# A third pair of feed-forward chunks as block products, on tokens without the norm's factor, in a transformer block on one core

## The chip, the cores and the metric

The kernel runs on one core of a Trainium2 chip. The metric is device time in microseconds of one launch. The profile is of one execution; its span, from the first to the last instruction of the engines, is a little shorter than the time of that execution. TensorE does the matmuls, ScalarE casts, copies and looks up activation functions, VectorE (DVE) does the elementwise work, GpSimd (POOL) some transfers and a little elementwise work, and SyncE (SP) issues most loads.

## The reference

One block over 256 tokens of 1024 channels, in fp32. The hidden width of a feed-forward is 2816.

```python
def rmsnorm(x, g):
    return x * rsqrt(mean(x * x) + 1e-6) * g

def swiglu(h, w_in, w_down):
    gate, up = split(h @ w_in, 2)
    return (silu(gate) * up) @ w_down

x = x + 0.5 * rmsnorm(swiglu(rmsnorm(x, g1), ffn1_w_in, ffn1_w_down), g2)
h = rmsnorm(x, g3)                                   # mixer
q_a, f_a, i_a, g_a, q_b, k_b, v_b, f_b, gates = split(h @ w_in)
a = rmsnorm(gated_recurrence(silu(q_a), f_a, i_a), g4) * silu(g_a)
b = forgetting_attention(q_b, k_b, v_b, f_b)
gA, gB = sigmoid(gates + b_gate)
x = x + rmsnorm((gA * (a @ w_branch_a) + gB * (b @ w_branch_b)) @ w_out, g5)
x = x + rmsnorm(memory_attention(rmsnorm(x, g6), rmsnorm(mem, g7)), g8)
x = x + 0.5 * rmsnorm(swiglu(rmsnorm(x, g9), ffn2_w_in, ffn2_w_down), g10)
```

## The kernel before

**Split weights.** Each product of two fp32 operands is three matmuls, of the high parts and low parts of both (high by high, high by low, low by high), summed in one bank. A weight unit is 128 x 1024 (512 KB). `load_split` has SP load it into a `raw` tile (4 buffers), ScalarE cast the high part `hi` (L137) and DVE subtract it for the low part `lo` (L138); 8 buffers each for `hi` and `lo`. The tokens stand transposed, in eight blocks of 128 channels x 256 tokens, as high and low part too (`hT`, `lT`, made by `gain_split` with the norm's gain, L271 and L272). The norm's factor per token (the rsqrt) is left out of them and multiplied in after the product, as `r2[h]` for the two halves h of 128 tokens.

**A feed-forward (`ffn`)** goes through 11 chunks (`NFF`) of 256 hidden columns. For an ordinary chunk, four units of `w_in` are met with each half of the tokens, 24 matmuls of 512 columns a half (`act_tok`; `act_first` does both halves side by side, for the first three chunks of the first feed-forward). `act_evac` then takes the Silu of the gate columns on ScalarE and multiplies it on DVE with the up columns to `at`. `flush` puts four transposes of `at` on TensorE and splits the result to `act`. `down(c, h)` multiplies `act` of chunk c and half h with two units of `w_down`, 12 matmuls of 512 columns into the accumulators `acc`, one or two chunks later.

**A pair of chunks as block products (`quad`).** Two chunks can be done together: tokens in 2 halves, channels in 2 halves and hidden columns in 2 chunks make a 2 x 2 by 2 x 2 block product, done with seven products of 12 matmuls in the place of eight. It needs sums of token blocks (`s1` to `s4`, made once by `mixed`) and four sums of weight blocks, T1 to T4. In the first feed-forward the half of the units that is only needed in sums is loaded into `wide` (2 buffers), and DVE makes the sums from `raw` and `wide`: `t1` (L481), `t2` (L482), `t4` (L484) for each half q of the channels, T3 later in place in `wide` (L494). `sum_of(k)` then splits a sum to high and low part (L156, L157). The order on TensorE in a pair is: 24 matmuls on two weight blocks, transposes of a chunk before it, T1's product, `down`, T2's product, `down`, T3's, `down`, and the rest. In the second feed-forward the sums were made between the feed-forwards and are loaded from DRAM. `QUADS_1 = (5, 8)` and `QUADS_2 = (3, 5, 7, 9)` name the first chunk of each pair.

Before the first pair, `mixed` (before) multiplies the tokens with the norm's factor, which must stand as a row: `row_of` makes it by two diagonal matrices and two matmuls with ones. The product of both is split anew to the pair `N`, and chunks behind it use `N` in place of `X` and no factor in `act_evac`.

**The order.** Each engine runs one queue in order; a scheduler lays out the queues from the order in which the program asks for work, with its priorities. `after(n)` puts an instruction right behind the n-th matmul of the program's own log and `issue_after` behind a given instruction. The loads on SP run in the order of the program, each as soon as its buffer is free.

**Start and end.** Eight loads (`head`, into the four `raw` and the two `wide` buffers) bring a block of tokens, of the first weights and the gains together; ScalarE (L713, L271) and DVE split them block by block. `norm_1` loads x and makes the norm's factors, with `rstd_x` for each half. The first feed-forward stands up to about 180 us in the span, mixer and memory attention to about 600, then the second feed-forward to about 775 and the last norm: `post_last` takes the Sqrt on ScalarE (L357), the reciprocal and two steps of a root's refinement on DVE, and updates x in three parts, two on DVE (L376) and one by ScalarE and POOL (L373 and on).

## Time and profile before

| | |
|---|---|
| time, median of 3 runs | 785.01 us (785.0 to 785.46) |
| the profiled execution | 785.17 us, span 783.4 us |
| TensorE (PE) busy | 774.3 us, 99% of the span |
| weight load (PEld) | 669.9 us, 86% |
| DVE | 646.2 us, 82% |
| ScalarE (ACT) | 468.4 us, 60% |
| POOL | 48.4 us, 6% |
| DMA | 193.61 MB, mean 247 GB/s |

How to read it: a row of a group names line, engine, operation, out<-in, shape, count, then busy time and mean ns of one, then idle time in front of it with what ended it. A row of the timeline has the start in us from the span's start, the duration, the engine, line and operation; a square bracket gives a wait before it and whom it was for; "x2" puts two like instructions in one row, and the duration runs to the end of the last. A row of the windows has start and end, the length, then for PE, PEld, DVE, ACT and POOL the busy time with the count of instructions, then the granted clock, the share of the DMA engines and GB/s. Matmul rows are those of one helper, L93 (`MM`), and are told apart by their tiles.

### The profile page before, as it was taken

How to read it: one execution, taken by the hardware profiler on the slowest of the kernel's cores; microseconds unless marked ns; L12 is line 12 of the kernel's file. 1: busy time of each engine (PE TensorE's matmuls, PEld its weight loads, DVE VectorE, ACT ScalarE, POOL GpSimd, SP SyncE). 2: the span in 40 equal slices, each digit the busy share in tenths (PEclk: the TensorE clock that was granted, in tenths of full speed). 3: DMA queues.
4: the chain of work that ended last, by engine and by line, in shares of the span. 5: the costliest groups of instructions: out<-in, count | busy, mean ns of one | idle time of the engine just before them, and what ended most of it. 6: DMA issues, size and time to landing. Idle time of an engine off the chain costs nothing.

```text
span 783.4 us, 13175 instructions
## 1 busy us (share of the span) xinstructions
PE 774.3 (99%) x5004; PEld 669.9 (86%) x5004; DVE 646.2 (82%) x1004; ACT 468.4 (60%) x704; POOL 48.4 (6%) x81
## 2 busy tenths in 40 slices
PE   9999999999999999999999999999999999999996
PEld 7888888888899999998888888999888888888884
DVE  7889989968798898578777886998787889888864
ACT  7665664756752447347674444744646758677763
POOL 0000000000121100200001221011110000000000
PEclk9999999999999999999999999999999999999999
DMA  9794484476687655753479999579875279899831
GB/s 349 249 327 154 155 309 161 147 233 245 251 305 257 183 191 164 232 212 121 152 278 341 377 338 378 203 275 375 319 226 185 83 261 388 311 314 323 339 122 54
DMA packets 57392, 193.61 MB, mean 247 GB/s; under 512 B 6249, under 2 KB 9713, under 8 KB 57329
## 3 DMA queue, kind: packets, MB, share of 16 engines
q1 hardware_dynamic: 48080, 159.60, 57.9%
q0 software_dynamic: 9104, 33.04, 12.1%
q8 instruction: 39, 0.64, 0.3%
q14 instruction: 25, 0.20, 0.1%
q10 hardware_dynamic: 144, 0.13, 0.0%
HBM read 174.92 MB, written 17.83 MB: 246 GB/s over the span
## 4 chain that ended last, share of the span: by engine, by line
PE 99%; ACT 0%; DVE 0%; issue 0%; DVEq 0%; ACTq 0%
PE mm L93 64%; PE acc L93 28%; PE tr L93 4%; PE tr L395 1%; PE tr L315 1%; PE tr L1067 0%; PE tr L1158 0%; PE tr L1264 0%; ACT L357 0%; PE tr L406 0%; DVEq L1393 0%; DVE xs L376 0%; ACT hT L156 0%; ACT y L357 0%; ACT junk L243 0%
## 5 line engine op out<-in xcount | busy, mean ns | idle before, releaser
L138 DVE TENSOR_TENSOR lo<-raw,hi 128x1024 fp32r<-128x1024 f32 (+1 forms) x228 | 271.3, 1205 | 53.0 <-ACT hi L137 49.2
L137 ACT CAST hi<-raw 128x1024 fp32r<-128x1024 f32 (+1 forms) x228 | 232.1, 1036 | 118.2 <-PE mm L93 69.5
L93 PE MATMUL mm<-lo,hT 128*128 128x512 f32 (+1 forms) x448 | 171.2, 386 | 0.0
L93 PE MATMUL mm<-hi,hT 128*128 128x512 f32 (+1 forms) x448 | 170.7, 385 | 0.0
L93 PE MATMUL mm<-hi,lT 128*128 128x512 f32 (+1 forms) x448 | 170.4, 384 | 0.0
L93 PE MATMUL acc<-hi,act 128*128 128x512 f32 x352 | 113.2, 391 | 0.0
L93 PE MATMUL mm<-hT,hi 128*128 128x256 f32 x384 | 109.0, 284 | 0.1
L93 PE MATMUL mm<-hT,lo 128*128 128x256 f32 x384 | 109.0, 284 | 0.0
L93 PE MATMUL mm<-lT,hi 128*128 128x256 f32 x384 | 108.9, 284 | 0.0
L93 PEld LDWEIGHTS mm<-hi,hT 128*128 128x128 f32 x448 | 84.1, 188 | 16.1 <-ACT hT L271 0.7
L93 PEld LDWEIGHTS mm<-hi,lT 128*128 128x128 f32 x448 | 84.1, 188 | 15.8 <-DVE lT L272 0.5
L93 PEld LDWEIGHTS mm<-lo,hT 128*128 128x128 f32 x448 | 84.0, 188 | 15.0 <-DVE lo L138 0.4
L93 PEld LDWEIGHTS acc<-hi,act 128*128 128x128 f32 x352 | 65.9, 188 | 13.7 <-DVE act L157 0.2
L93 PEld LDWEIGHTS mm<-hT,hi 128*128 128x128 f32 x384 | 73.6, 192 | 0.5 <-issue 0.3
L93 PEld LDWEIGHTS mm<-lT,hi 128*128 128x128 f32 x384 | 73.6, 192 | 0.1
L93 PEld LDWEIGHTS mm<-hT,lo 128*128 128x128 f32 x384 | 73.6, 192 | 0.1
L93 PE MATMUL acc<-lo,act 128*128 128x512 f32 x176 | 69.0, 392 | 0.0
L157 DVE TENSOR_TENSOR lo<-wide,hi 128x1024 fp32r<-128x1024 f32 x40 | 47.9, 1219 | 1.5 <-ACT hi L156 1.1
L156 ACT CAST hi<-wide 128x1024 fp32r<-128x1024 f32 x40 | 41.5, 1052 | 11.5 <-DVE wide L494 7.5
L776 POOL DMA_DIRECT2D sums<-wide x32 | 23.6, 738 | 357.8 <-DVE wide L773 240.8
L93 PEld LDWEIGHTS acc<-lo,act 128*128 128x128 f32 x176 | 33.1, 188 | 6.7
L93 PE MATMUL mm<-hi,sh 128*128 128x512 f32 x96 | 37.5, 390 | 0.0
(243 smaller groups left out, 1126.8 us busy)
## 6 DMA issues: line engine op xcount, KB each, us to landing
raw<-in_wts_dram SPq DMA_DIRECT2D x232, 512.0 KB, 5.1
sums<-wide POOLq DMA_DIRECT2D x32, 512.0 KB, 6.2
wide<-sums SPq DMA_DIRECT2D x32, 512.0 KB, 6.9
wide<-in_wts_dram POOLq DMA_DIRECT2D x28, 512.0 KB, 6.7
wide<-in_wts_dram SPq DMA_DIRECT2D x12, 512.0 KB, 6.4
raw<-in_gf_dram SPq DMA_DIRECT2D x12, 344.0 KB, 4.9
head<-in_head_dram SPq DMA_DIRECT2D x8, 388.0 KB, 5.7
grow<-in_rows_dram SPq DMA_DIRECT2D x4, 512.0 KB, 8.9
```

Source lines behind the costliest of these rows:

```text
L93: log.append(PE.matmul(*args, **kw).ins)
L137: S.copy(h, r)
L138: V.tensor_tensor(out=l, in0=r, in1=h.bitcast(F32), op=ALU.subtract)
L156: S.copy(hi, src)
L157: V.tensor_tensor(out=lo, in0=src, in1=hi.bitcast(F32), op=ALU.subtract)
L315: PE.transpose(ps[:, j * P : (j + 1) * P], src(kb), ident)
L395: PE.transpose(trv[:, j, h * P : (h + 1) * P], ats[c, h][:, j * P : (j + 1) * P], ident)
L776: G.dma_start(sums[u][2 * e : 2 * e + 2, q, :, i * 512 : i * 512 + 512].rearrange("k p n -> p k n"), W[:, e])
```

## The change

- `QUADS_1` has three pairs, (3, 6, 9), in place of two, (5, 8). The eleven chunks are then 0, 1, 2, a pair, 5, a pair, 8, a pair. The last pair is at the end, as in the second feed-forward, and `ffn` treats the end of the first one as it did that of the second (which `down` is left for last differs).
- `mixed` takes the tokens without the norm's factor. `row_of`, the multiplication and the split to `N` are gone from it; it returns the sums alone. `act_evac` always has the factor as Silu's scale and in DVE's product. In the first feed-forward the whole tokens, `full1`, are eight copies by ScalarE out of the `head` tiles, with the gain as scale, asked for behind the last head's low part; in the second, DVE adds high and low part as before.
- In a pair of the first feed-forward `t2` and `t4` of the first half (q = 0) are asked for at once, those of the second half behind the first `down`.
- Smaller: both halves' norm factors are made together (`rstd_pair`, 128 x 2 in place of 128 x 1); the row of gains for the last norm is loaded later; q and G of the mixer take ScalarE's Silu in place of Sigmoid and a product on DVE; in the second feed-forward the Sqrt table is asked for only behind the last Silu of the program (before: behind the Silu of the second half of chunk 10, after which another Silu came); `post_last` has three updates on DVE.

```diff
-QUADS_1 = (5, 8)
+QUADS_1 = (3, 6, 9)
-    def mixed(X, r, back=0):
-        with after(len(log) - 1 - back):
-            row = row_of(r)
-        full = [m4([P, 4, T], n="full") for _ in range(2)]
-        for f, xh, xl in zip(full, X.h, X.l):
-            V.tensor_tensor(out=f, in0=xh.bitcast(F32), in1=xl.bitcast(F32), op=ALU.add)
-            V.tensor_tensor(out=f, in0=f, in1=bc(row, [P, 4, T], 1), op=ALU.mult)
-        N = Pair()
-        for q in range(2):
-            split(N.h[q], N.l[q], full[q])
+    def mixed(X, full):
+        if full is None:
+            full = [m4([P, 4, T], n="full") for _ in range(2)]
+            for f, xh, xl in zip(full, X.h, X.l):
+                V.tensor_tensor(out=f, in0=xh.bitcast(F32), in1=xl.bitcast(F32), op=ALU.add)
...
+    full1 = [m4([P, 4, T], n="full") for _ in range(2)]
+    for kb in range(KB):
+        with tc.issue_after(lo_last):
+            S.activation(full1[kb // 4][:, kb % 4], heads[kb][:, :T], AF.Copy, scale=heads[kb][:, T + 512 + kb : T + 512 + kb + 1])
...
         def act_evac(ps, c, h):
-            if mix:
-                silu = S.activation(sg, ps[:, :FC], AF.Silu)
-            else:
-                silu = S.activation(sg, ps[:, :FC], AF.Silu, scale=r2[h])
-            if c == NFF - 1 and (c, 1 - h) in ats and not first_half:
+            silu = S.activation(sg, ps[:, :FC], AF.Silu, scale=r2[h])
+            if len(ats) == 2 * NFF - 1 and not first_half:
                 with tc.issue_after(silu.ins):
                     S.activation(warm, ones[:, 0:1], AF.Sqrt)
...
+                def rest(W, raws, t1, t2, t4):
+                    V.tensor_tensor(out=t2, in0=t1, in1=W[:, :, 1], op=ALU.add)
+                    for i in range(2):
+                        V.tensor_tensor(out=t4[:, i], in0=t2[:, i], in1=raws[i][:, 512:], op=ALU.add)
...
-                    V.tensor_tensor(out=t2, in0=t1, in1=W[:, :, 1], op=ALU.add)
-                    for i in range(2):
-                        summed = V.tensor_tensor(out=t4[:, i], in0=t2[:, i], in1=raws[i][:, 512:], op=ALU.add).ins
+                        summed = V.tensor_tensor(out=t1[:, i], in0=raws[i][:, :512], in1=W[:, i, 0], op=ALU.add).ins
+                    if q == 0:
+                        rest(W, raws, t1, t2, t4)
...
             down(n_down, 0)
+            if not sums:
+                rest(W, raws, t1, t2, t4)
...
-            down(n_down + 1, 1)
+            if not (last and first_half):
+                down(n_down + 1, 1)
...
-            for c in ends:
+            for c in (NFF - 3, *ends) if done == NFF - 2 else ends:
                 down(c, 1)
...
-        for eng, a, b, queue in ((G, 512, 768, nc.scalar), (V, 0, 512, nc.sync), (V, 768, 1024, nc.sync)):
+        for a, b, queue in ((0, 512, nc.sync), (512, 768, nc.scalar), (768, 1024, nc.sync)):
...
-            if eng is G:
-                S.activation(t, t, AF.Copy, scale=r)
-                G.tensor_tensor(out=xh, in0=t, in1=xh, op=ALU.add)
-            else:
-                V.scalar_tensor_tensor(out=xh, in0=t, scalar=r, in1=xh, op0=ALU.mult, op1=ALU.add)
+            V.scalar_tensor_tensor(out=xh, in0=ts[a // 512][:, a % 512 : a % 512 + b - a], scalar=r, in1=xh, op0=ALU.mult, op1=ALU.add)
```

In all TensorE has 16 instructions fewer, and DVE seven.

**ScalarE at the start, before.** The rows show its queue from the last head tile (`head_94`: high part of the weights, of the tokens) to the first casts of chunk 1 (`raw_203`, `raw_209`):

```order
L713 CAST hi_143<-head_94 128x512
L271 ACTIVATE hT_87<-head_94 128x256
L713 CAST hi_143<-head_94 128x512
L271 ACTIVATE hT_87<-head_94 128x256
L137 CAST hi_204<-raw_203 128x1024
L137 CAST hi_210<-raw_209 128x1024
```

The same place after, where `full_153` and `full_154` are the two halves of the whole tokens:

```order
L725 ACTIVATE full_153<-head_89 128x256
L719 CAST hi_143<-head_94 128x512
L285 ACTIVATE hT_87<-head_94 128x256
L725 ACTIVATE full_153<-head_90 128x256
L719 CAST hi_143<-head_94 128x512
L285 ACTIVATE hT_87<-head_94 128x256
L725 ACTIVATE full_153<-head_91 128x256
L725 ACTIVATE full_153<-head_92 128x256
L725 ACTIVATE full_154<-head_93 128x256 x2
L725 ACTIVATE full_154<-head_94 128x256 x2
L136 CAST hi_214<-raw_213 128x1024
```

All eight copies stand ahead of the first cast of chunk 1 (`hi_214`), two of them between the splits of the last heads.

**DVE in the first pair, before** (chunks 5 and 6). `sum_787`, `sum_788` and `sum_789` are t1, t2 and t4 of q = 0, `sum_810` to `sum_812` those of q = 1; `lo_819` and `lo_823` are the low parts of T1:

```order
L482 TENSOR_TENSOR sum_788<-sum_787,wide_772 128x1024
L422 SCALAR_TENSOR_TENSOR at_729<-mm_702,rstd_317,sg_727 128x256
L484 TENSOR_TENSOR sum_789<-sum_788,raw_773 128x512
L484 TENSOR_TENSOR sum_789<-sum_788,raw_780 128x512
L157 TENSOR_TENSOR lo_807<-raw_803,hi_806 128x1024
L481 TENSOR_TENSOR sum_810<-raw_796,wide_795 128x512
L481 TENSOR_TENSOR sum_810<-raw_803,wide_795 128x512
L157 TENSOR_TENSOR lo_819<-sum_787,hi_818 128x1024
L482 TENSOR_TENSOR sum_811<-sum_810,wide_795 128x1024
L157 TENSOR_TENSOR lo_823<-sum_810,hi_822 128x1024
```

The same place after (chunks 3 and 4). `sum_502` to `sum_504` are the sums of q = 0, `sum_525` is t1 of q = 1, `wide_487` and `wide_510` in place are T3, `act_330` the low part of chunk 2's activations, `lo_531` and `lo_535` the low parts of T1:

```order
L465 TENSOR_TENSOR sum_503<-sum_502,wide_487 128x1024
L498 TENSOR_TENSOR wide_487<-wide_487 128x2x512
L467 TENSOR_TENSOR sum_504<-sum_503,raw_488 128x512
L467 TENSOR_TENSOR sum_504<-sum_503,raw_495 128x512
L156 TENSOR_TENSOR lo_522<-raw_518,hi_521 128x1024
L485 TENSOR_TENSOR sum_525<-raw_511,wide_510 128x512
L485 TENSOR_TENSOR sum_525<-raw_518,wide_510 128x512
L156 TENSOR_TENSOR lo_531<-sum_502,hi_530 128x1024
L498 TENSOR_TENSOR wide_510<-wide_510 128x2x512
L156 TENSOR_TENSOR act_330<-tr_565,act_330 128x512
L156 TENSOR_TENSOR lo_535<-sum_525,hi_534 128x1024
```

`t2` of q = 1 has moved out from between T1's two low parts, and both T3, with one `act`, now stand ahead of the second of them.

**ScalarE at the end, before.** `sg` are Silus, `warm` the call that fetches the Sqrt table, `y` the Sqrt of the last norm:

```order
L417 ACT_TABLE_LOAD
L417 ACTIVATE warm_79<-ones 128x1
L412 ACT_TABLE_LOAD
L412 ACTIVATE sg_8073<-mm_7823 128x256
L156 CAST act_7787<-tr_8077 128x2x128
L156 CAST act_7786<-tr_8130 128x2x128
L243 ACTIVATE junk,ss_1577_8135<-acc_6913 128x512
L243 ACTIVATE junk,ss_1577_8135<-acc_6914 128x512
L243 ACTIVATE junk,ss_1587_8184<-acc_6915 128x512
L243 ACTIVATE junk,ss_1587_8184<-acc_6916 128x512
L357 ACT_TABLE_LOAD
L357 ACTIVATE y_8191<-ss_1587_8184,v_8186 128x1
```

The same place after:

```order
L415 ACTIVATE sg_8018<-keep_7903,rstd_6529 128x256
L415 ACTIVATE sg_8045<-mm_7796,rstd_6705 128x256
L155 CAST act_7760<-tr_8050 128x2x128
L418 ACT_TABLE_LOAD
L418 ACTIVATE warm_79<-ones 128x1
L155 CAST act_7759<-tr_8103 128x2x128
L257 ACTIVATE junk,ss_1560_8108<-acc_6886 128x512
L257 ACTIVATE junk,ss_1560_8108<-acc_6887 128x512
L257 ACTIVATE junk,ss_1570_8157<-acc_6888 128x512
L257 ACTIVATE junk,ss_1570_8157<-acc_6889 128x512
L366 ACTIVATE y_8164<-ss_1570_8157,v_8159 128x1
```

The table load in front of the Sqrt is gone; the Sqrt table is fetched once, behind the last Silu.

67 lines of the change are left out of this document (37 added, 30 removed).

## The prediction

> **What bounds the kernel now.** First the page: the busy line and the chain that ended last.
>
> ```profile
> PE 774.3 (99%) x5004; PEld 669.9 (86%) x5004; DVE 646.2 (82%) x1004; ACT 468.4 (60%) x704; POOL 48.4 (6%) x81
> PE 99%; ACT 0%; DVE 0%; issue 0%; DVEq 0%; ACTq 0%
> ```
>
> TensorE has work nearly all the time and the chain runs on it. A busy TensorE can still hide short waits, so next the windows by stage (x counts instructions) and the timeline of TensorE in the first feed-forward.
>
> ```profile
> 4.00:180.00 176.00, 175.98 (x797) 144.72 (x797) 152.40 (x200) 110.57 (x148) 0.00 (x0) 1.00 0.66 228
> 600.00:775.00 175.00, 175.00 (x796) 143.80 (x795) 146.51 (x202) 119.66 (x166) 0.00 (x0) 1.00 0.69 248
> 62.11 0.40 PE L93 MATMUL mm<-hi,hT 128*128 128x512 f32 x1
> 73.02 0.39 PE L93 MATMUL acc<-hi,act 128*128 128x512 f32 x1
> ```
>
> Both feed-forwards are gapless at granted clock 1.00. Between the two matmuls lie 48 matmuls of 512 columns: 10.91 / 48 = 0.227 us each. So a matmul removed is worth 0.227 us, and any wait that the change brings to TensorE is paid in full. DVE, at 152.4 of 176 us (87%) in the first feed-forward, is the engine that could bring one.
>
> **The change part by part.**
>
> *Matmuls.* A pair of chunks as block products needs 7 x 12 = 84 matmuls in place of 4 x 24 = 96; the third pair therefore removes 12: 12 x 0.227 = **2.72 us**. Tokens without the norm's factor need no broadcast row of it; the two rows that `mixed` made (one per feed-forward) go. Each stands on TensorE like this:
>
> ```profile
> 55.74 0.61 PE L93 MATMUL tr<-diag,ones 128*128 128x128 f32 x4
> 56.11 0.47 PE L93 MATMUL acc<-hi,act 128*128 128x512 f32 x1
> ```
>
> 56.11 - 55.74 = 0.37, twice **0.74 us**. Both terms are sure: 16 matmuls fewer stand on TensorE, and nothing hides work there. [...]
>
> *The tail.* The last Silu now comes before the Sqrt table is fetched, so the table stays, and POOL's share of the last update goes to DVE.
>
> ```profile
> 776.27 0.19 ACT L243 ACTIVATION_READ_ACCUMULATOR junk<-acc 128x1 f32 x1
> 776.49 1.28 ACT L357 ACT_TABLE_LOAD   x1
> 777.11 0.15 DVE L359 TENSOR_TENSOR v<-ss,v 128x1 f32<-128x1 f32 x1
> 777.78 0.29 ACT L357 ACTIVATE y<-ss,v 128x1 f32<-128x1 f32 x1
> 778.11 0.17 DVE L364 RECIPROCAL y<-y 128x1 f32<-128x1 f32 x1 [0.85 <-ACT y L357]
> 778.76 1.61 DVE L376 SCALAR_TENSOR_TENSOR xs<-post,y,xs 128x512 f32<-128x512 f32 x2
> L376 DVE SCALAR_TENSOR_TENSOR xs<-post,y,xs 128x256 f32<-128x256 f32 x1 | 0.9, 946 | 0.0
> L422 DVE SCALAR_TENSOR_TENSOR at<-mm,rstd,sg 128x256 f32<-128x256 f32 x12 | 5.7, 476 | 0.5 <-ACT sg L414 0.4
> ```
>
> Without the load y is ready at 776.8, but DVE only ends v at 777.26; the reciprocal starts at 777.28 in place of 778.11, a gain of 0.83, not 1.28. The update then has three DVE instructions (0.67 to the start of the second, 0.40 more, then 0.48: 1.55) for two that took 1.61 beside POOL. Together **0.9 us** (0.6 to 1.1). [...]
>
> *Start.* ScalarE now also copies the eight token blocks (`full1`), all ahead of the first cast of chunk 1.
>
> ```profile
> 8.16 0.51 ACT L271 ACTIVATE hT<-head 128x256 fp32r<-128x256 f32 x1
> 8.59 0.62 ACT L713 CAST hi<-head 128x512 fp32r<-128x512 f32 x1
> 12.06 0.51 ACT L271 ACTIVATE hT<-head 128x256 fp32r<-128x256 f32 x1
> 12.82 1.05 ACT L137 CAST hi<-raw 128x1024 fp32r<-128x1024 f32 x1 [0.25 <-DMA raw<-in_wts_dram]
> 13.90 5.07 DVE L138 TENSOR_TENSOR lo<-raw,hi 128x1024 fp32r<-128x1024 f32 x4 [0.53 <-ACT hi L137]
> 16.20 0.62 PE L93 MATMUL acc<-hi,hT 128*128 128x512 f32 x2
> 17.10 0.62 PE L93 MATMUL acc<-lo,hT 128*128 128x512 f32 x2
> ```
>
> Such a copy occupies ScalarE 0.43 (8.16 to 8.59). ScalarE is free at 12.06 + 0.43 + 8 x 0.43 = 15.93; the cast ends at 16.98 where TensorE wants it at 16.20 (0.8 late); the low part takes DVE 1.22 more, 18.24 for 17.10: **+1.1 us**. The load behind the cast now waits for the copy of its buffer (about 11.0) and lands by 16.1 at the latest (landing times below), so it adds at most 0.2; behind it on SP's queue wait the loads of chunks 1 and 2 and of x, all wanted more than 4 us later than they land. Bounds 0.8 to 1.4. The second unit is wanted 2.7 us later and is in time.
>
> *The first pair, two chunks earlier.* DVE's order there is all work without a break; its prices, from the first pair of before:
>
> ```profile
> 70.58 0.68 DVE L157 TENSOR_TENSOR act<-tr,act 128x512 fp32r<-128x512 f32 x1
> 71.18 0.47 DVE L422 SCALAR_TENSOR_TENSOR at<-mm,rstd,sg 128x256 f32<-128x256 f32 x1
> 71.57 1.28 DVE L481 TENSOR_TENSOR sum<-raw,wide 128x512 f32<-128x512 f32 x2
> 72.77 1.22 DVE L157 TENSOR_TENSOR lo<-raw,hi 128x1024 fp32r<-128x1024 f32 x1
> 73.91 1.21 DVE L482 TENSOR_TENSOR sum<-sum,wide 128x1024 f32<-128x1024 f32 x1
> 75.04 0.47 DVE L422 SCALAR_TENSOR_TENSOR at<-mm,rstd,sg 128x256 f32<-128x256 f32 x1
> 81.25 1.21 DVE L157 TENSOR_TENSOR lo<-sum,hi 128x1024 fp32r<-128x1024 f32 x1
> 84.35 0.40 PE L93 MATMUL mm<-hi,sh 128*128 128x512 f32 x1
> 38.90 0.40 PE L93 MATMUL acc<-hi,act 128*128 128x512 f32 x1
> ```
>
> Start to start: 1.14 for 1024 elements, 0.60 for 512, 0.40 for 256. In before the second low part of T1 is there at 82.5; TensorE, at its eighth matmul behind 84.35, wants it at 85.9: 3.4 us to spare. In the new program chunk 2 ends at 38.90 + 1.1 = 40.0; 24 matmuls of `down` and the pair's first 24 with 4 transposes (0.35) bring TensorE to T1 at 51.3, and to its second low part, behind four matmuls of `down`, at 53.8. DVE reaches chunk 2's first gate product no sooner than 40.8 and, by the loads, at 41.7; from there to the start of that low part it has six of 1024 (two low parts of weights, one of T1, one t2, both T3), six of 512 (one t1 of q = 0, two t4, two t1, `act`) and two of 256: 6.84 + 3.6 + 0.8 = 11.2. The low part ends at 41.7 + 11.2 + 1.2 = 54.1, 0.4 late (54.17 for 53.8 unrounded). From its start to the end of T2's second low part DVE has five more of 1024, three of 512 and one of 256, 5.7 + 1.8 + 0.4 = 7.9, so 62.0; TensorE comes there 32 matmuls (7.26) behind 53.8, at 61.06: **1.0 us** late in all. Behind it stand four `down` matmuls whose weights are there, and DVE catches up.
>
> The 41.7 hangs on loads:
>
> ```profile
> raw<-in_wts_dram SPq DMA_DIRECT2D x232, 512.0 KB, 5.1
> DMA to landing us min/median/max: 3.5/3.8/5.1
> 30.03 2.35 DVE L138 TENSOR_TENSOR lo<-raw,hi 128x1024 fp32r<-128x1024 f32 x2
> 35.92 1.06 ACT L137 CAST hi<-raw 128x1024 fp32r<-128x1024 f32 x1 [0.73 <-DMA raw<-in_wts_dram]
> 37.26 1.05 ACT L137 CAST hi<-raw 128x1024 fp32r<-128x1024 f32 x1 [0.29 <-DMA raw<-in_wts_dram]
> ```
>
> A unit lands 3.5 to 5.1 us after its issue, and 1.34 behind the one before it (35.92, 37.26). Chunk 2's last low part frees a buffer at 32.4 in before, about 32.7 in the new order; the pair's second unit is issued then, third in a row of loads, and is there at 38.3 (37.6 to 39.5). So the stall lies between 0.1 (DVE at 40.8) and 2.2; I take 1.0.
>
> *The rest at nothing.* The second and third pair follow an ordinary chunk each, as before's second did without a gap; t2 and t4 of the half q = 1, now behind two low parts, leave DVE earlier for those, and the loads for the second `down` wait for weights' low parts, not for t4. The first feed-forward's end takes the second one's order, gapless to 775. The added Silu table load (1.28 on ScalarE, which is at 234 of 420 us between the feed-forwards) is covered; without cover it would cost 1.28. Fewer DVE instructions for q, G and `mixed` meet no wait of TensorE. I allow -0.3 to +0.8.
>
> **The sum**, against the profiled execution, 785.17 us (span 783.4 and 1.77 around it, which stays): -2.72 - 0.74 - 0.9 + 1.1 + 1.0 = -2.2, so 782.95. That execution stands 0.16 above the median 785.01; the forecast is **782.8 us**, its own range 781.3 to 784.6.
>
> **The rivals.**
>
> *No new stall.* ScalarE's copies fall into its waits and DVE keeps ahead: -4.36, 780.7. For it: ScalarE waits for loads in the first 60 us. Against: not between 8 and 12.5, where the copies stand. Chance 0.12.
>
> *The first pair starves for loads.* Its eight units come at 249 GB/s, as the second window did, not at 1.34 us each:
>
> ```profile
> 20.00:40.00 20.00, 20.00 (x93) 16.55 (x93) 16.22 (x33) 12.94 (x20) 0.00 (x0) 1.00 0.75 249
> ```
>
> 524 KB / 249 = 2.1 us, eight times 0.76 more = 6 us, of which some 4 lie in DVE's lead: 2 to 3 more of stall, 784.8 to 786.0, say 785.4. Against it: that window was held by buffers, not by the DMA engines (share 0.75). Chance 0.16.
>
> *Slower: DVE becomes the bound of the first feed-forward.* A third pair adds to DVE six lows (6 x 1.14), sums of 9.4 (four t1, two t2, four t4, two T3) and three of 512 (1.8): 18.0; `mixed` gives back six of 1024 and a second chain of the norm, 8.8. The net 9.2 us must fit in 176 - 152.4 = 23.6 of idle time, less 3.5 for the shorter stage. If only the part x fits, TensorE waits 9.2 - x beyond the 4.36 gained; slower than 786.6 once less than 3.3 fits, and 789.9 if nothing does. For it: pairs now stand in a row with one chunk between them, and much of DVE's idle time lies where casts are late. Against: a pair with the chunk behind it is 24 low parts (27.4), the sums (9.4), six of 512 (3.6) and six of 256 (2.4), 43 us of DVE, in 204 matmuls of TensorE, 46. Chance 0.10.
>
> **How the numbers follow.** Forecast 0.62, the rivals 0.12, 0.16, 0.10. The range 780.9 to 786.0 leaves out half of the first, a little of the second and all of the third, under 0.2. A measurement here can tell 0.2%, 1.57 us, from no change: under 783.44 is faster. That holds for the first rival and about 0.72 of the forecast: 0.57. Same: 0.28 x 0.62 + 0.13 = 0.30. Slower: 0.10 + 0.03 = 0.13.
>
> **What would show it.** In the new trace: chunk 1's first matmul at 17.0, its first low part some 1.1 us late; T1 of the first pair near 51.3 with small gaps to T2, their sum about 1; no gap in the second and third pair; Sqrt right behind the last square sum and the span's last DVE instruction 3 us before its end. Gaps above 2 us in the first pair, casts waiting for raw, mean the loads; gaps in every pair with DVE full mean the third rival; a chunk 1 at 16.2 means the first.

## The result, and the profile after

The changed kernel takes **788.48 us** (median of 6, 786.78 to 790.64) where the kernel before took 784.99 beside it: ratio 1.0044, 95% interval 1.0034 to 1.0055. It is slower by 3.5 us; 782.8 was forecast, in a range of 780.9 to 786.0. Its profiled execution took 787.54 us, span 785.8, 2.4 more than the span before.

First the page after, the busy line and the chain that ended last:

```profile
PE 772.8 (98%) x4984; PEld 665.8 (85%) x4984; DVE 647.1 (82%) x998; ACT 475.3 (60%) x715; POOL 48.1 (6%) x80
PE 87%; DVE 5%; DMA 3%; ACT 2%; issue 1%; SPq 0%; DVEq 0%; ACTq 0%
```

TensorE does less, as it should (20 matmul records fewer, 4984 for 5004: 12 of the pair and eight of the factor's rows, whose four fp32 matmuls have two records each in the trace). But the chain, which ran on TensorE alone before, now leaves it for DVE, DMA and ScalarE. TensorE's waits after (who waits for whom: us in total, times, longest):

```profile
PE mm L92 <- issue: 2.1, 1, 2.1
PE mm L92 <- DVE lo L156: 1.3, 2, 1.1
PE tr L92 <- DVE ones L205: 1.1, 1, 1.1
PE acc L92 <- ACT hi L136: 0.8, 2, 0.6
PE tr L410 <- DVE at L420: 0.3, 1, 0.3
```

Before, only the third of them was there. This list does not hold all that is lost: from 40 to 60 TensorE is idle for 1.63 us (20.00 - 18.37) and yet 13 matmuls, 3.0 us, behind the kernel before. So the windows are needed too (x in the second column counts TensorE's matmuls). First before, then after:

```profile
0.00:20.00 20.00, 18.91 (x81) 15.60 (x82) 14.24 (x25) 15.30 (x27) 0.71 (x6) 1.00 0.93 351
40.00:60.00 20.00, 20.00 (x93) 16.58 (x93) 16.63 (x19) 11.45 (x15) 0.00 (x0) 1.00 0.94 332
```

```profile
0.00:20.00 20.00, 18.22 (x74) 14.25 (x75) 13.51 (x27) 14.92 (x28) 0.70 (x6) 1.00 0.79 271
40.00:60.00 20.00, 18.37 (x80) 13.74 (x78) 18.65 (x24) 10.61 (x14) 0.00 (x0) 1.00 0.46 174
```

Seven matmuls fewer by 20 us (7 x 0.227 = 1.6) and 13 fewer from 40 to 60 (3.0), where the first pair stands. To divide the whole, the same places of the program on the timelines: the mixer's first product, the start of the second feed-forward and the last matmul, before:

```profile
186.32 0.39 PE L93 MATMUL mm<-hi,hT 128*128 128x512 f32 x1
596.34 1.29 PE L315 MATMUL tr<-ident,xs 128*128 128x128 f32 x8
775.29 0.39 PE L93 MATMUL acc<-hi,act 128*128 128x512 f32 x1
```

After, with chunk 1's first matmul and the first `down` (before: 16.20 and 38.90) ahead of them:

```profile
17.27 0.73 PE L92 MATMUL acc<-hi,hT 128*128 128x512 f32 x2 [0.56 <-ACT hi L136]
40.49 0.40 PE L92 MATMUL acc<-hi,act 128*128 128x512 f32 x1
189.00 0.39 PE L92 MATMUL mm<-hi,hT 128*128 128x512 f32 x1
600.23 1.29 PE L324 MATMUL tr<-ident,xs 128*128 128x128 f32 x8
778.33 0.39 PE L92 MATMUL acc<-hi,act 128*128 128x512 f32 x1
```

| stage | forecast | this execution |
|---|---|---|
| matmuls and row taken from the first feed-forward | -3.1 | -3.1 |
| start, to the first `down` | +1.1 | +1.6 |
| first pair (13 matmuls from 40 to 60) | +1.0 | +3.0 |
| rest of the first feed-forward | 0 | +1.2 |
| mixer and memory (410.02 to 411.23) | 0 | +1.2 |
| second feed-forward (178.95 to 178.10) | -0.4 | -0.85 |
| from the last matmul to the end (8.11 to 7.47) | -0.9 | -0.65 |
| sum | -2.3 | +2.4 |

(The prediction gives its own sum as -2.2; its terms make -2.26.) The median lies 0.9 above this execution, and single executions lie 3.9 apart, against 0.9 of the kernel before; only this one of the six was profiled.

**Start.** SP's queue before and after, the loads of chunk 1:

```profile
5.70 4.04 SPq L136 DMA_DIRECT2D raw<-in_wts_dram  x4
```

```profile
11.66 3.44 SPq L135 DMA_DIRECT2D raw<-in_wts_dram  x4
13.78 2.50 ACT L725 ACTIVATE full<-head 128x256 f32<-128x256 f32 x6
16.18 1.03 ACT L136 CAST hi<-raw 128x1024 fp32r<-128x1024 f32 x1
18.20 1.05 ACT L136 CAST hi<-raw 128x1024 fp32r<-128x1024 f32 x1 [0.99 <-DMA raw<-in_wts_dram]
```

The first cast of chunk 1 stands behind six copies and ends at 17.21, and TensorE waits for it. The copies also hold the raw buffers, so the loads start 6 us later: the second cast waits 0.99 us for its load.

**First pair.** ScalarE's first and last cast of its four raws after, DVE's first gate product of chunk 2, its low parts of the last raw and of T1, and TensorE's longest wait:

```profile
38.28 1.05 ACT L155 CAST hi<-raw 128x1024 fp32r<-128x1024 f32 x1 [1.53 <-DMA raw<-in_wts_dram]
...
46.02 1.05 ACT L155 CAST hi<-raw 128x1024 fp32r<-128x1024 f32 x1 [1.16 <-DMA raw<-in_wts_dram]
44.28 0.48 DVE L420 SCALAR_TENSOR_TENSOR at<-mm,r,sg 128x256 f32<-128x256 f32 x1
50.28 1.22 DVE L156 TENSOR_TENSOR lo<-raw,hi 128x1024 fp32r<-128x1024 f32 x1
52.62 1.21 DVE L156 TENSOR_TENSOR lo<-sum,hi 128x1024 fp32r<-128x1024 f32 x1
55.49 1.21 DVE L156 TENSOR_TENSOR lo<-sum,hi 128x1024 fp32r<-128x1024 f32 x1
51.55 0.50 PE L92 MATMUL mm<-lo,hT 128*128 128x512 f32 x1 [1.11 <-DVE lo L156]
```

The raws come 2.6 us apart (7.74 for three steps; the DMA engines' share was 1.01 to 1.03 from 38 to 44, with a wide load beside each raw), and the last one's low part waits 3.2 us more on DVE, behind the sums of the first half.

**Mixer.** The wait with no releaser stands right behind a burst of small matmuls; the line of the page is a DMA queue of instructions (packets, MB, share):

```profile
268.59 1.29 PE L92 MATMUL acc<-q,k 128*32 128x16 f32 x128
271.96 0.32 PE L92 MATMUL mm<-hi,lT 128*128 128x344 f32 x1 [2.08 <-issue]
q8 instruction: 39, 0.64, 0.3%
```

39 packets for 4984 matmul records and as many weight loads: 0.64 MB / 39 is 16.4 KB, and 4984 / 39 is 128 matmul records, a packet. That the packets hold TensorE's instructions is the author's estimate from this count. One of them starts at 269.52, 0.36 us ahead of the wait (269.88 to 271.96).

### The profile page after: what moved, and what is told of

Its sections match the earlier page's. It is cut to its first block, busy times and chain, and to the rows that moved or that the text cites. A ratio compares the mean times of both kernels' runs of the same rounds, so it can differ in the third digit from the quotient of the medians.

```text
span 785.8 us, 13132 instructions
## 1 busy us (share of the span) xinstructions
PE 772.8 (98%) x4984; PEld 665.8 (85%) x4984; DVE 647.1 (82%) x998; ACT 475.3 (60%) x715; POOL 48.1 (6%) x80
## 4 chain that ended last, share of the span: by engine, by line
PE 87%; DVE 5%; DMA 3%; ACT 2%; issue 1%; SPq 0%; DVEq 0%; ACTq 0%
PE mm L92 59%; PE acc L92 22%; PE tr L92 3%; DMA raw<-in_wts_dram 2%; DVE lo L156 2%; PE tr L324 1%; PE tr L399 1%; DMA head<-in_head_dram 1%; DVE lo L137 1%; ACT hi L136 1%; DVE sum L467 0%; DVE at L420 0%; DVE sum L465 0%; DVE sum L485 0%; DVE act L156 0%
## 5 line engine op out<-in xcount | busy, mean ns | idle before, releaser
L137 DVE TENSOR_TENSOR lo<-raw,hi 128x1024 fp32r<-128x1024 f32 (+1 forms) x220 | 261.1, 1201 | 57.6 <-ACT hi L136 53.9
L136 ACT CAST hi<-raw 128x1024 fp32r<-128x1024 f32 (+1 forms) x220 | 223.9, 1035 | 126.0 <-PE mm L92 65.7
L92 PE MATMUL mm<-hi,lT 128*128 128x512 f32 (+1 forms) x424 | 161.0, 384 | 2.1 <-issue 2.1
L92 PE MATMUL mm<-lo,hT 128*128 128x512 f32 (+1 forms) x424 | 161.9, 385 | 1.1 <-DVE lo L156 1.1
L92 PE MATMUL mm<-hi,hT 128*128 128x512 f32 (+1 forms) x424 | 161.4, 384 | 0.0
L92 PEld LDWEIGHTS mm<-hi,hT 128*128 128x128 f32 x424 | 79.6, 188 | 17.4 <-issue 2.3
L92 PEld LDWEIGHTS mm<-lo,hT 128*128 128x128 f32 x424 | 79.5, 188 | 15.5 <-DVE lo L156 1.5
L92 PEld LDWEIGHTS mm<-hi,lT 128*128 128x128 f32 x424 | 79.5, 188 | 14.9 <-DVE lT L286 0.5
L92 PE MATMUL mm<-lo,sh 128*128 128x512 f32 x112 | 44.0, 392 | 0.2 <-DVE lo L156 0.2
L92 PE MATMUL mm<-hi,sh 128*128 128x512 f32 x112 | 44.0, 393 | 0.0
```

What stands on the lines that cost most here:

```text
L92: log.append(PE.matmul(*args, **kw).ins)
L136: S.copy(h, r)
L137: V.tensor_tensor(out=l, in0=r, in1=h.bitcast(F32), op=ALU.subtract)
```

## The experiments

All are edits of the changed kernel unless another is named. "Loss" is TensorE's time beyond its matmuls.

| run | median us (range) | ratio to before, 95% interval |
|---|---|---|
| early copies | 786.43 (784.70 to 791.51) | 1.0024 (1.0004 to 1.0045) |
| no copies | 787.25 (784.87 to 788.14) | 1.0026 (1.0015 to 1.0038) |
| late rest | 804.51 (803.20 to 810.62) | 1.0262 (1.0221 to 1.0303) |
| wide first | 800.16 (797.62 to 803.26) | 1.0193 (1.0166 to 1.0221) |
| no copies, less DVE | 783.94 (781.65 to 789.30) | 0.9984 (0.9965 to 1.0002) |
| no copies, pairs (5, 8) | 785.14 (783.22 to 788.00) | 1.0001 (0.9988 to 1.0014) |
| no copies, pairs (6, 9) | 785.51 (783.00 to 788.43) | 1.0004 (0.9990 to 1.0018) |
| no copies, five raw buffers | 785.82 (784.10 to 786.91) | 1.0001 (0.9991 to 1.0010) |
| 16 records more | 787.61 (786.99 to 789.14) | 1.0028 (1.0017 to 1.0040) |
| before, 112 records more | 792.04 (791.74 to 792.60) | 1.0084 (1.0069 to 1.0099) |
| no copies, five raw buffers, 16 records more | 782.38 (781.80 to 783.65) | 0.9963 (0.9948 to 0.9977) |
| no copies, pairs (5, 8), 4 records more | 783.66 (782.23 to 784.90) | 0.9977 (0.9968 to 0.9987) |
| no copies, 16 records more | 785.77 (784.70 to 786.55) | 1.0008 (0.9998 to 1.0017) |
| before, 106 records more | 786.22 (784.43 to 792.62) | 1.0028 (1.0007 to 1.0049) |
| no copies, six raw buffers, 16 records more | 792.43 (789.23 to 793.84) | 1.0086 (1.0061 to 1.0112) |

### The copies of the tokens

**Early copies.**

```diff
-    for kb in range(KB):
-        with tc.issue_after(lo_last):
-            S.activation(full1[kb // 4][:, kb % 4], heads[kb][:, :T], ...)
+        if kb < 4:            # in the loop over the heads
+            copy_of(kb)
...
+        with tc.issue_after(casts[3]):      # behind chunk 1's casts
+            for kb in range(4, KB):
+                copy_of(kb)
```

> The changed kernel with its eight whole-token copies moved on ScalarE: the four out of raw buffers each right behind its own head's split, the four out of wide buffers behind the casts of chunk 1. In the profile of the changed kernel the loads of chunk 1 are issued from 11.66 us (before: 5.70), since the copies hold the four raw buffers; TensorE then loses 1.6 us in chunk 1, 3.3 in the first pair and 0.9 in the third. Theory 'held buffers': loads run from about 7 us again, chunk 1 begins near 16.3, the first pair's casts wait less and its stall falls from 3.3 to under 1: 788.5 - 1.5 - 2.5 = 784.5 (783.5 to 785.2). Theory 'pair too wide for the DMA' (eight units of 512 KB in a row, 2.6 us for each raw with its wide): only the start comes back, 787.0. Theory 'DVE's order' (sums of the first half stand ahead of the last raw's low part): also only the start, 787.0.

786.43, 2 us better but neither theory's number. The first `down` came at 39.81 in place of 40.49. But a new wait stood in chunk 5. ScalarE and two windows of this run:

```profile
92.10 1.04 ACT L156 CAST hi<-raw 128x1024 fp32r<-128x1024 f32 x1 [2.93 <-DMA raw<-in_wts_dram]
93.05 0.58 ACT L156 CAST act<-tr 128x512 fp32r<-128x512 f32 x1
92.00:96.00 4.00, 2.32 (x6) 1.80 (x7) 2.34 (x3) 2.92 (x4) 0.00 (x0) 0.71 0.10 40
96.00:100.00 4.00, 4.00 (x17) 3.29 (x16) 4.00 (x7) 0.03 (x1) 0.00 (x0) 0.87 0.00 0
```

The cast of the second pair's last raw waits 2.93 us for its load, and the cast of the first pair's activations stands behind it; TensorE waits 2.3 us for that, and the granted clock falls (0.71 and 0.87 in these windows; it is 0.50 from 93.6 to 97.1). In the changed kernel TensorE was late enough there not to notice.

**No copies.**

```diff
-    ffn("f1_in", "f1_dn", X1, full1, norm_1, 0, 0, QUADS_1, None, first)
+    ffn("f1_in", "f1_dn", X1, None, norm_1, 0, 0, QUADS_1, None, first)
```

> The changed kernel without ScalarE's copies: the first feed-forward's whole tokens are two DVE additions of high and low part (128x1024), as in the second one. Theory 'held buffers': raw buffers come free at 5.7 us as in the kernel before; like the run with early copies, 784.5 or up to 1 better or worse (two more DVE additions, 2.3 us, ahead of the first pair). Theory 'pair too wide for the DMA': 787.0. Theory 'DVE's order': the 2.3 us of DVE are paid in the first pair: 787.0 to 789.3.

787.25, though its profiled execution took 784.87. The start's loss is gone (first `down` at 39.25); the first pair still loses 2.2 us and chunk 5 with the second pair 1.7. With the 16 records of below in both, the copies are worth 787.61 - 785.77 = 1.8 us (1.5 if each run is taken against the kernel before that ran beside it): in total about what the start lost.

### What holds up the first pair

**Late rest.**

```diff
-                    if q == 0:
-                        rest(W, raws, t1, t2, t4)
+                    rests.append((W, raws, t1, t2, t4))
...
-                rest(W, raws, t1, t2, t4)
+                for a in rests:
+                    rest(*a)
```

> The changed kernel with t2 and t4 of both halves asked for behind the first down of a pair, where the changed kernel asks for those of the first half at once. In its first pair 3.6 us of DVE work (t2, T3 and t4 of the first half) stand between the last raw's cast (ready at 47.07) and its low part (50.28). Theory 'DVE's order': the first pair's stall of 3.3 us falls to under 1, the rest stays: 786.0. Theories 'held buffers' and 'pair too wide': the casts still come 2.6 us apart, T1's sums depend on the last load, and T2's sums are now late: the stall moves behind T1, 787.5 to 789; raw buffers held longer could make later loads late: up to 790.

804.51, far out of every expectation. TensorE's wait in this run:

```profile
PE acc L92 <- ACT hi L136: 14.9, 4, 6.3
```

t4 reads the raws, so all four raw buffers were held until behind the first `down`, and the next `down`'s weights could not be loaded: SP issued the pair's last raw at 37.72 and the next raw only at 56.81, after waiting for the sums t4. The run says nothing on the order on DVE; it says that raw buffers are what the loads hang on.

**Wide first.**

```diff
                 outs = act_first(c, mm)      # chunk 2
+                if quads[0] == 3:
+                    wides[3] = wide_loads(3)
...
-                        loads.append(nc.sync.dma_start(W[:, i].rearrange("p j n -> p (j n)"), wts[u]).ins)
```

> The changed kernel with the four wide loads of each pair ahead of its raw loads on SP's queue, those of the first pair right behind chunk 2's loads (wide buffers are free by then). Theory 'pair too wide for the DMA, wide and raw in turn on one queue': the raws land 1.3 us apart in place of 2.6, the first pair's stall falls from 3.3 to under 1: 786.0; the start's 1.6 us stay. Theory 'held buffers': what was lost at 5.7 to 11.7 us stays lost and the stall only shrinks by a part: 786.5 to 788. Theory 'DVE's order': 788.5, as the changed kernel.

800.16. The last three raws stood ready one behind the other, and the last one's cast ended at 45.0, 2.1 us sooner than in the changed kernel. T1 still waited, since its low parts now stood on DVE behind an `act` that waited until 52.39:

```profile
42.05 2.95 ACT L155 CAST hi<-raw 128x1024 fp32r<-128x1024 f32 x3
53.00 2.35 DVE L156 TENSOR_TENSOR lo<-sum,hi 128x1024 fp32r<-128x1024 f32 x2
54.27 0.50 PE L92 MATMUL mm<-lo,sh 128*128 128x512 f32 x1 [2.33 <-DVE lo L156]
```

Loads that came sooner did not help here, but DVE's order changed with them, so the run does not decide between the theories. In the rest of the 12 us are waits of 2.5 and 2.7 us without a releaser and a clock down to 0.53 behind the latter, with the other pairs' loads in a new order too, so the total is not divided further.

**Less DVE.**

```diff
-                    for i in range(2):                                  # t4
+                    for i in range(0 if c == 3 else 2):
...
-                        V.tensor_tensor(out=W[:, :, 0], in0=W[:, :, 0], in1=W[:, :, 1], op=ALU.add)    # T3
+                        if c > 3:
+                            V.tensor_tensor(out=W[:, :, 0], in0=W[:, :, 0], in1=W[:, :, 1], op=ALU.add)
```

> The run without copies (787.25 us, its profiled execution 784.87), and in its first pair alone four additions for t4 and the two for T3 left out (t2 and the raw half stand in their place, so this leaves out part of the computation): 4.7 us of DVE. In the run without copies DVE works without a break from 39.32 to 63.1 and TensorE loses 2.2 us in the first pair, 1.7 in chunk 5 and the second pair. Theory 'DVE is the bound of the first pair': its 2.2 us go, 785.0 (784.5 to 785.6). Theory 'loads': the last raw's cast waits for its load as before, nothing changes there: 786.7 to 787.3.

This edit stands on the run without copies. In the first pair it leaves out four additions for t4 and two for T3 and takes t2 and the raw half in their place, so part of the computation is missing. 783.94, 3.3 below the run without copies. The window of the first pair, without copies and then with less DVE:

```profile
40.00:60.00 20.00, 19.76 (x88) 15.53 (x87) 20.00 (x26) 10.83 (x14) 0.00 (x0) 1.00 0.51 183
```

```profile
40.00:60.00 20.00, 20.00 (x92) 16.53 (x91) 19.96 (x24) 14.23 (x18) 0.00 (x0) 1.00 0.62 224
```

DVE is full in both; with 4.7 us taken from it TensorE has no gap, and the wait in chunk 5 went as well. So without copies DVE's amount of work in the first pair is what TensorE pays for there. By the prediction's own prices the pair alone has 34.5 us of DVE (18 low parts 20.5, sums 9.4, five of 512 elements 3.0, four of 256 1.6), where TensorE's 132 matmuls and the transposes take 31; a pair needs a lead of DVE, and behind chunk 2 the loads leave too little.

How the changed kernel's loss divides shows when its runs are laid side by side, matmul record by matmul record, from the first `down` on (two of these runs follow below):

| run | last cast of the four raws starts, us | 180th record, us behind the first `down` | loss in the first pair |
|---|---|---|---|
| no copies, less DVE (no gap, the measure for the others) | 43.07 | 40.41 | 0 |
| no copies, five raw buffers, 16 records more | 41.85 | 42.41 | 2.0 |
| no copies, six raw buffers, 16 records more | 41.4 | 42.41 | 2.0 |
| no copies | 43.42 | 42.67 | 2.3 |
| changed kernel | 46.02 | 43.61 | 3.2 |

Of the 3.2 us (3.0 by the windows, which end at 60) some 1.2 go with earlier loads. The other 2.0 stay although the loads come 4 us earlier, and go when DVE has less to do. The runs without copies have two more additions on DVE (2.3 us), but ahead of the pair: with five raw buffers DVE still stood idle for 0.57 us at 35.5 and for 0.58 at 39.8.

**Pairs (5, 8) and (6, 9).**

```diff
-QUADS_1 = (3, 6, 9)
+QUADS_1 = (5, 8)
```

> The run without copies with the pairs of the kernel before, (5, 8): tokens without the factor, the new tail, Silu for q and G, but no third pair and no pair at chunk 3. Theory 'the early first pair costs it' (DVE and loads have no lead at chunk 3): no stall is left but those of before, 785.0 - 0.74 (two rows of the factor) - 0.65 (tail) = 783.6 (783.2 to 784.2), steady from run to run. Theory 'the unnormed tokens or the new mixer cost it' (waits that come with the rest of the change): 785 or more.

> As the run with pairs (5, 8), with pairs (6, 9): the changed kernel's second and third pair without its first. Theory 'the early first pair costs it': 783.6, as with (5, 8). Theory 'a pair at the end costs it too' (TensorE lost 0.9 us in the changed kernel's third pair): 784.3 to 784.8. If three pairs were bound by DVE's sum over the stage alone, this is below both and steady as well.

785.14 and 785.51, above 783.6, but from 783.0 to 788.4 in single executions. In the two profiled ones (784.54, 783.00) the first feed-forward had no wait behind chunk 1, with a pair at its end too. So the unnormed tokens and the last pair cost TensorE nothing here; something behind them varies.

**Five raw buffers.**

```diff
-        raw = wp.tile([P, D], F32, tag="raw", name=nm("raw"), bufs=4)
+        raw = wp.tile([P, D], F32, tag="raw", name=nm("raw"), bufs=5)
...
-    mp = ctx.enter_context(tc.tile_pool(name="data", bufs=21))
+    mp = ctx.enter_context(tc.tile_pool(name="data", bufs=20))
```

> The run without copies with five raw buffers in place of four (and 20 data buffers in place of 21). In the run without copies the fourth raw of the second pair waits for a buffer, lands at 88.9, and its cast holds up the cast of chunk 3's activations behind it on ScalarE: TensorE waits 1.1 us at 90.5 (2.3 in the run with early copies). Theory 'loads': both this wait and part of the first pair's 2.2 us go: 784.5 (784.0 to 785.5). Theory 'DVE is the bound of the first pair': only the wait at 90.5 goes, 786.0.

785.82. The wait in chunk 5 is gone, the first pair still loses 2.0 us: as the theory of DVE's bound has it. The profiled execution had a wait of the mixer's kind, which took one matmul off the end of a burst, and the granted clock fell behind it (0.50 from 269.9 to 273.3, which these two windows cut in the middle):

```profile
265.56 1.28 PE L92 MATMUL acc<-q,k 128*32 128x16 f32 x127
269.18 0.20 PE L92 MATMUL acc<-q,k 128*32 128x16 f32 x1 [2.34 <-issue]
268.00:272.00 4.00, 2.82 (x12) 2.80 (x13) 2.13 (x5) 0.00 (x0) 2.17 (x6) 0.74 0.75 285
272.00:276.00 4.00, 4.00 (x24) 4.00 (x23) 0.00 (x0) 1.42 (x2) 0.10 (x1) 0.84 0.02 7
```

### The wait in the mixer

Among the changed kernel and its edits with three pairs, that wait stood at the end of the second burst in five of seven profiles (2.1 to 2.6 us). With pairs (6, 9), which have 12 matmuls more ahead of it, it stood some ten records earlier in the burst and was short:

```profile
265.82 1.21 PE L92 MATMUL acc<-q,k 128*32 128x16 f32 x118
267.27 0.30 PE L92 MATMUL acc<-q,k 128*32 128x16 f32 x10 [0.24 <-issue]
```

So it seems to move with the count of instructions, not with the place in the program. The change took 16 records away ahead of this place. At 128 records a packet that shifts the borders between packets against the bursts; that the wait hangs on these borders is an estimate of the author's from the two counts (in the expectations, the theory 'instruction block').

All traces together (with the runs below) show where the wait stands against the packets. The packet is the one of the instruction queue that is moved nearest to the start of the second burst:

| profile | packet's start against the burst's, us | wait in or behind the burst | wait's end behind the packet's start |
|---|---|---|---|
| changed kernel | +0.9 | 2.08 | 2.44 |
| late rest | +1.3 | 2.25 | 2.22 |
| no copies, five raw buffers | +1.4 | 2.34 | 2.22 |
| wide first | +1.5 | 2.50 | 2.32 |
| no copies, less DVE | +1.6 | 2.61 | 2.32 |
| no copies, pairs (6, 9) | -0.9 | 0.24 | 2.35 |
| the eleven others, the kernel before among them | -1.3 to -3.2 | none | |

Eight shorter waits without a releaser elsewhere in the mixer (0.20 to 0.99 us) end 2.35 to 2.67 us behind the start of such a packet too. That is all 14 in the mixer; the 2.7 us of the run with wide loads first, at 195, stands 20 us from any packet and is of another kind. The author takes the 14 for waits for that packet, though the profile names no releaser. What sets the packet's place is less clear: early copies and no copies have the changed kernel's 4984 records, and theirs came 1.6 and 1.3 ahead of the burst.

**16 records more**, on the changed kernel, on the run with five raw buffers, on the run without copies, and 4 on the one with pairs (5, 8) (eight, eight, eight and two of these fp32 matmuls):

```diff
     for _ in range(WARM):
         MM(wps[:, :P], ones, ones, start=True, stop=True)
+    for _ in range(8):
+        MM(wps[:32, :16], ones[:, :32], ones[:, :16], start=True, stop=True)
```

> The changed kernel with eight tiny matmuls of ones (16 matmul records, 0.01 us each) behind the warm-up matmuls, nothing else. In its profile TensorE stands 2.08 us at 269.88 to 271.96 right behind a burst of 128 small matmuls (1.29 us) with nothing that releases it, and one packet of the queue 'instruction' (16 KB, 39 in the run) is moved at 269.5. [...] Sixteen more put the borders where the kernel before has them: no such wait, runs closer together, 788.5 - 2.3 = 786.2 (785.4 to 786.8). Theory 'the wait is another, from loads or the new Silu in the mixer': 788.5 and the wait stays.

> The run with five raw buffers and no copies (785.82 us, its profiled execution 786.26 with a wait of 2.34 us at 269.2 and a clock of 0.74 and 0.84 in the 8 us behind it), with eight tiny matmuls (16 records) behind the warm-up. Theory 'instruction block': the wait and the clock's fall go, 784.0 (783.3 to 784.6), under the kernel before. Theory 'another wait': 785.8.

> The run without copies and with pairs (5, 8) (785.14 us, single executions from 783.2 to 788.0), with two tiny matmuls (4 records) behind the warm-up, as many as the first row of the factor had. Theory 'instruction block': the borders stand as in the kernel before, the spread narrows to some 783.2 to 784.5, median 783.6. Theory 'another wait': 785.1 with the same spread.

> The run without ScalarE's copies (787.25 us) with eight tiny matmuls (16 records) behind the warm-up, so that it differs from the changed kernel with those (787.61) only in the copies, and from the run with five raw buffers and those (782.38) only in the buffers. Theory 'held buffers': the copies cost the start's 1.6 us and 1 us of the first pair: 785.0 (784.4 to 785.6). Theory 'DVE and buffers': the copies only cost what the start shows, and the first two pairs stay as they are: 786.0 to 786.6.

787.61, 782.38, 783.66 and 785.77. In none of the four profiles does the wait stand at the second burst (the longest without a releaser is 0.44, in the third). The medians are lower than without the records (by 0.9, 3.4, 1.5 and 1.5), and their executions lie 1.9 to 2.7 us apart in place of 2.8 to 4.8. With five raw buffers and with pairs (5, 8) the intervals of the ratios lie apart; for the changed kernel and the run without copies they overlap. With pairs (5, 8) the packet came 1.3 ahead of the burst without the records and 1.4 with them, so the profiles do not show why that run gained. The changed kernel itself gained less than the 2.3 expected: its profiled execution lost more in the first feed-forward (190.44 against 189.00 at the mixer's first product), which is not where the records stand; its mixer took 410.14 in place of 411.23. The page of the run with five raw buffers and 16 records more, where TensorE is nearly the whole chain again:

```profile
PE 97%; DVE 2%; issue 0%; ACT 0%; DVEq 0%; ACTq 0%
```

This one beats both kernels: 0.9963 of the kernel before, 3.0 us. From 785.77 to 782.38 there is only the fifth raw buffer (for a data buffer): 3.4 us, or 3.7 if each is taken against the kernel before beside it.

**The same in the kernel before.**

```diff
-WARM = 8
+WARM = 5
...
+    for _ in range(59):
+        MM(wps[:32, :16], ones[:, :32], ones[:, :16], start=True, stop=True)
```

> The kernel before with 59 tiny matmuls (118 records) behind five in place of eight warm-up matmuls (6 records fewer): 112 records more, which with blocks of 128 puts the borders where the changed kernel has them (16 fewer). Theory 'instruction block': a wait of 2 to 2.6 us for nothing that the profile shows appears behind the second burst near 268, and the time goes from 785.2 to 787.3 to 789.5, with a wider spread. Theory 'the wait belongs to the change': 785.2, no wait.

792.04, but not for the reason expected. The records took 8.9 us with the warm-up, and five of the 6.7 us lie at the start (the first product at 9.90 in place of 4.87). At the second burst no wait stood; the packet had come 2.1 us ahead of it, so the count had not put the border where it was to go:

```profile
1.07 8.91 PE L93 MATMUL tr<-ones 128*128 128x128 f32 x128 [1.07 <-DVE ones L206]
```

The second try had six warm-up matmuls and 55 small ones in four column groups, as in the bursts:

```diff
+    for i in range(55):
+        c, o = i % 4, i // 4 * 16
+        MM(wps[32 * c : 32 * c + 32, o : o + 16], ones[:, :32], ones[:, :16], start=True, stop=True, tile_position=(0, 32 * c))
```

> The kernel before with 55 tiny matmuls in four column groups (110 records, 0.01 us each) behind six in place of eight warm-up matmuls (4 records fewer): 106 records more, which with blocks of 128 moves the borders as 22 records fewer would, to the start of the second burst of small matmuls (its instruction packets start 3.3 us ahead of that burst at present, and 0.9 us behind the burst's start in the changed kernel). Theory 'instruction block': a wait of 1.5 to 2.6 us without a releaser appears at the end of the second burst near 268 us, time 785.3 + 2 = 787 (786.5 to 789.5), spread wider. Rival: the wait comes with the change's other parts: 785.3 to 785.6 (0.2 for the later start) and no such wait.

786.22, and single executions up to 790.45 and 792.62, where the kernel before had 784.25 to 786.06 beside it. So small matmuls at the start alone make that kernel slower and unsteady. But its profiled execution (785.67) was a mild one: the packet came 1.6 us ahead of the second burst, and it shows only two short waits, in other places of the mixer:

```profile
PE acc L93 <- issue: 0.4, 1, 0.4
PE mm L93 <- issue: 0.3, 1, 0.3
```

The traces show that the 14 waits end 2.2 to 2.7 us behind the start of a packet, and four profiles that with 16 (or 4) records more none stands at the second burst; of the four medians two speak for it. That TensorE waits for the packets, and that the count of records sets where, is argued from this and not shown: in neither of these two runs did the count put the packet behind the burst's start, and none of the long executions of the second was profiled.

**Six raw buffers** (and 19 data buffers), with the 16 records:

> The run with five raw buffers and the tiny matmuls (782.38 us), with six raw buffers and 19 data buffers. TensorE still loses about 2.2 us in its first pair there. Theory 'loads': more buffers bring the raws of the first pair earlier, 781.0 to 781.8. Theory 'DVE is the bound of the first pair': as with five, 782.2 to 782.6; fewer data buffers could cost a wait, up to 783.5.

792.43, outside both. The first feed-forward was as with five, matmul by matmul, which speaks for DVE's bound, but a new wait stood at 407.5, and the granted clock behind it was 0.50 from 408.6 to 412.0. That the fewer data buffers brought it is likely and not shown:

```profile
PE mm L92 <- ACT junk L257: 3.9, 1, 3.9
```

## Why the prediction was wrong, step by step

*Matmuls and rows, -3.46*: right. With the other losses gone it comes back: the run with five raw buffers and 16 records more reaches the mixer at 185.71, 0.6 ahead of the kernel before, in spite of the first pair's loss of 2.0 us.

*Tail, -0.9*: right in mechanism. Sqrt follows the last square sum (its end is at 779.50) with no table load:

```profile
779.54 0.29 ACT L366 ACTIVATE y<-ss,v 128x1 f32<-128x1 f32 x1
780.21 0.15 DVE L373 RECIPROCAL y<-y 128x1 f32<-128x1 f32 x1
780.85 1.54 DVE L380 SCALAR_TENSOR_TENSOR xs<-post,y,xs 128x512 f32<-128x512 f32 x3
```

DVE's last update ends 4.06 us behind the last matmul's start, 5.08 before; the span's end gained 0.65 in this execution and 1.0 in the run with five raw buffers and 16 records more.

*Start, +1.1*: right in mechanism, mis-sized, 1.6 by the first `down`. Chunk 1's first matmul stood at 17.27 where 17.0 was forecast, its first low part at 18.59 where 18.24 was, and by the second unit's first matmul (20.52, before 18.92) the whole 1.6 was lost. The second unit was in time, as forecast, but only by its slack: its cast waited 0.99 us for a load that the held buffers had put off, which the forecast did not have, and ended at 19.25.

*The first pair, +1.0*: the step that failed. It took units to land 1.34 us apart, from an ordinary chunk; in the pair a wide load of the same size goes with each raw, and the raws came 2.6 us apart. The pair's second raw was to be there at 38.3, and its cast could start only at 40.86. So DVE came to chunk 2's first gate product at 44.28 and not 41.7. From there on the forecast's list of DVE's work held: to T1's second low part 11.21 us where 11.2 was summed (55.49, not 52.9), and T2's second low part ended at 64.57, again 2.6 later than the 62.0 forecast.

A second step of the forecast failed that this delay hides: that early loads would leave only 0.1, with DVE at 40.8 (0.8 behind the first `down`), and that behind T2 the weights of `down` are there and DVE catches up. In the run with five raw buffers and 16 records more DVE came to that gate product 0.96 behind the first `down` (39.48), where the forecast's sum would leave some 0.3. The pair still lost 2.0, in gaps of up to 0.6 spread over the pair; one of them, 0.30, was a wait for the weights of `down`:

```profile
40.44 0.47 DVE L420 SCALAR_TENSOR_TENSOR at<-mm,r,sg 128x256 f32<-128x256 f32 x1
```

Less work for DVE closed these gaps; earlier loads alone did not. The rival "starves for loads" had this size, 2 to 3 us more, at 0.16; the third rival had DVE as the bound, at 0.10, and its sign. Each had a part of it: loads take away DVE's lead, and without enough lead the pair is bound by DVE. The argument against the third rival, 43 us of DVE in 46 of TensorE, is an average over pair and chunk; in the pair alone it is 34.5 in 31.

*The rest at nothing*: failed, by 1.2 us in the first feed-forward. The third pair's end waited for a gate product (0.32 at 170.26), and where the first pair ran earlier, chunk 5 paid for the second pair's loads; the remainder is not traced wait by wait. The second feed-forward gained 0.45 more than its row of the factor, which is not traced either. *The mixer* had no term at all for what moved it most: 2.08 us without a releaser, which ended 2.44 us behind the start of a packet of instructions; without it the mixer would have taken 409.15, so it costs more than the 1.2 of the table shows. Wait-free runs passed the mixer in 409.1 to 410.2 us (410.02 before), so the new Silu cost nothing, as assumed.

## What to carry to other kernels

An average by stage hides a bound: where a piece of work alone asks more of an engine than the bound engine gives it time, count the lead with which that engine enters it, and what takes the lead away (here buffers held six microseconds longer, and two loads where one was counted). A buffer held by a cheap copy (six took 2.50 us here) costs what its next load was to feed (loads 6 us later, a cast 0.99 us late), not the copy. When the executions of a kernel lie further apart after a change, look in the traces for waits that end behind a transfer, those of instructions among them (2.08 us, 2.44 behind a packet's start, here), before arguing over the median; the fifth buffer was worth more here than the third pair.

## What was not expected of the hardware

In the changed kernel the instruction queue moved 39 packets of 16.4 KB, one for 128 of the 4984 matmul records. In the five profiles where such a packet began to move 0.9 to 1.6 us behind the start of the second burst (128 matmuls in 1.3 us), TensorE waited 2.1 to 2.6 us with no releaser in the profile, and all 14 waits without a releaser in the mixers of all profiles ended 2.2 to 2.7 us behind the start of a packet.

Behind waits of 2.25 to 2.61 us in four profiles (late rest, early copies, five raw buffers, less DVE) the granted clock was 0.50 for 3.4 us and 1.00 again after it, which costs some 1.7 us more (the author's estimate, 0.50 x 3.4). Behind the waits of 2.08 us in the changed kernel and 2.50 us in the run with wide loads first it stayed at 1.00, so the length of the wait alone does not decide.
